# Loading and multiplying the last-but-one pair's down weights ahead of the last pair's gate-and-up weights

## Chip, cores and metric

The kernel runs on one core of one Trainium2 chip. The metric is device time in microseconds (us) of one execution. All matrix products here are in float32; TensorE is the matrix engine, VectorE and ScalarE do elementwise work, and SyncE issues nearly all loads.

## The reference

One decoder layer on 256 tokens of width 1024: a gated mixer, then a mixture of 32 experts with the best four for each token, then a final RMSNorm. The change lies in the experts:

```python
def expert_block(args):
    xb, e = args
    gu = xb @ w_gu[e] + b_gu[e]              # 1024 x 2048 weights
    gate, up = jnp.split(gu, 2, axis=-1)
    gate = jnp.minimum(gate, SWIGLU_LIMIT)
    up = jnp.clip(up, -SWIGLU_LIMIT, SWIGLU_LIMIT)
    glu = gate * jax.nn.sigmoid(SWIGLU_ALPHA * gate)
    return ((up + 1.0) * glu) @ w_down[e] + b_down[e]   # 1024 x 1024 weights
...
y_assign = ys[dest] * w_sorted[:, None]
out = jax.ops.segment_sum(y_assign, sorted_tok, num_segments=n_tok)
...
return rms_norm(x, final_g)
```

Every expert's weights are read once: 8 MB of gate-and-up and 4 MB of down weights each, 12 MB for an expert and 24 MB for a pair of them (MB here is 2^20 bytes, as in the issue sizes of the profile).

## The kernel before

The 32 experts are taken in 16 pairs, numbered 0 to 15 (`NP` is 16). The 128 rows of the matrix engine's output are four groups of 32 tokens, shared between the two experts of a pair.

For each pair the program does these steps, each a function of its own:

- `gate_up(p)` multiplies the gathered tokens with the pair's gate-and-up weights, in eight blocks k of 128 rows, into four PSUM banks, and adds the bias from two small matmuls a bank (`add_bias`).
- `swiglu(pg)` is eight VectorE operations and two ScalarE sigmoids on those banks. Its result is `act`.
- `transpose_act` turns `act` on TensorE (two groups of four transposes) and ScalarE copies each group into `actT`.
- `down(p)` multiplies `actT` with the pair's down weights; each finished bank goes through VectorE into `yv`.
- `weigh(p)` (VectorE) and `turn_weights(p)` (TensorE, ScalarE) make the matrix `owT[p]` that sends rows back to tokens, and `scatter(owT[p])` multiplies it with `yv`, piece by piece, and VectorE adds each piece to the residual stream `xt`.

All engines run their instructions in the order in which the program emits them. The order is skewed by one pair: in the loop, `weigh`, `turn_weights` and `transpose_act` of pair p-1 come first, then `gate_up(p)` (with the scatter of pair p-2 after block 0, and the gathering of the next pair's tokens between the blocks), then `swiglu` of pair p is emitted, and `down(p-1)` follows. So TensorE multiplies the down weights of pair p-1 while VectorE and ScalarE do the SwiGLU of pair p.

The weights pass through a ring of seven places of 2 MB each (`RING`, `CHUNK_ELEMS`). A chunk of two places (4 MB: two blocks k of gate-and-up weights for both experts, or half of a pair's down weights) goes into one of three double positions in turn; the seventh place is only for chunks of one place. The list of loads (`add_gu2`, `add_dn`) is issued in order by SyncE from line 177; each waits until TensorE has finished with the chunk that held its place (`passed`). Loads of pair p: four chunks of gate-and-up weights, then two chunks of the down weights of pair p-1, in whole rows: `(k, n) == (4, D)` in `dn_rows` gives four rows of 1024 floats, 16 KB in one run, to each partition.

The end differs. The down weights of pair 14 are loaded after the last gate-and-up weights, as four chunks of one place, each with half of the columns (512 floats, runs of 2 KB). `down(14, ahead)` is emitted after `swiglu` of pair 15, and `ahead` puts between its four chunks: `weigh(15)`, then the transposes of pair 15 (into a buffer `aT` of its own) and half of the scatter of pair 14, then `turn_weights(15)`. The other half of that scatter follows, then `down(15, meanwhile, aT)`, whose weights come in four chunks of one place with 512 or 256 columns in a run, and in which `meanwhile` puts the scatter of pair 15 and the sums of squares of the final norm. The rest of the final norm and the output ends the program.

The lines of the profile: 1337 is a matmul of `gate_up` or `down` (banks `abank`, `cbank`), 1354 the bias, 1304 and 1305 the transposes of `act` and their copies, 1318 and 1320 `turn_weights`, 1327 and 1270 `scatter`, 1290 to 1296 SwiGLU, 1312 `weigh`, 1393 the write of `yv`.

Of the kernel before, what the change touches and what calls it, by code (L numbers as in the profile page):

```python
# [20 lines left out]
D = 1024  # L21
KB = D // P
T = 256
TT = T // P
FF = 1024
NE = 32
TOPK = 4
NP = NE // 2
# [48 lines left out]
def trunk(ctx: ExitStack, tc: tile.TileContext, x, c, norm1_g, ada_w, ada_b, w_in, gmlp_norm_g, gmlp_ws,  # L77
# [98 lines left out]
    def load(dst, src):  # L176
        nc.sync.dma_start(dst, src)  # L177
# [101 lines left out]
    def add_dn(p, *slots):  # L279

        dn_ids[p] = []

        def fn(t, parts):
            off = 0
            for k0, k, c0, n in parts:
                for e in range(2):
                    v = t[:, off:off + k * n]
                    load(v if (k, n) == (4, D) else v.rearrange("p (k n) -> p k n", k=k), dn_rows(wdn[2 * p + e], k0, k, c0, n))
                    off += k * n
        for parts in slots:  # L290
            size = sum(2 * a[1] * a[3] for a in parts) // CHUNK_ELEMS
            i = add(lambda t, parts=parts: fn(t, parts), None, size)
            off = 0
            for a in parts:
                dn_ids[p].append((i, off, a is parts[-1]) + a)
                off += 2 * a[1] * a[3]

    for p in range(NP):
        for j in range(KB // 2):
            if (p, 2 * j) not in EXTRA:  # L300
                add_gu2(p, j)
            elif p == 0:
                for i in range(2):
                    add_gu(p, 2 * j + i)
            if (p, j) == (0, 1):
                for pk_ in EXTRA:
                    if pk_[0]:
                        add_gu(*pk_)
        if p:
            add_dn(p - 1, *([[(4 * j, 4, 0, D)] for j in range(2)] if p < NP - 1 else  # L310
                            [[(k, 4, c, 512)] for c in (0, 512) for k in (0, 4)]))
    add_dn(NP - 1, [(0, 4, 0, 512)], [(4, 2, 0, 512), (6, 2, 0, 512)], [(0, 4, 512, 256), (4, 4, 512, 256)],
           [(0, 4, 768, 256), (4, 2, 768, 256), (6, 2, 768, 256)])

# [117 lines left out]
    def half(h):  # L432
        return slice(h * 512, (h + 1) * 512)
# [601 lines left out]
    n = len(steps)  # L1035
    done = live = at = room = 0
    for i in range(n + 1):
# [5 lines left out]
        if i < n:  # L1043
# [5 lines left out]
            while spread and room >= spread[0][0]:  # L1049
                c, f = spread.pop(0)  # L1050
# [79 lines left out]
    wk = {"g2b": big.tile([P, D], F32, name="x4", bufs=2)}  # L1130
# [154 lines left out]
    def swiglu(pg, a=None):  # L1285

        a = wk["act"] if a is None else a
        gs, us_ = [wk["sg"]() for _ in range(2)], [wk["su"]() for _ in range(2)]
        for h in range(2):
            V.tensor_scalar(gs[h], pg[h], LIMIT, None, op0=OP.min)  # L1290
            S.activation(a[:, half(h)], gs[h], AF.Sigmoid, scale=ALPHA)
            V.tensor_scalar(us_[h], pg[2 + h], LIMIT, -LIMIT, op0=OP.min, op1=OP.max)
        for h in range(2):
            s, g, u = half(h), gs[h], us_[h]
            V.scalar_tensor_tensor(u, u, 1.0, g, op0=OP.add, op1=OP.mult)
            V.tensor_tensor(a[:, s], u, a[:, s], op=OP.mult)

    def transpose_act(a=None, aT=None):
        a = wk["act"] if a is None else a
        aT = wk["actT"] if aT is None else aT  # L1300
        for b in range(2):
            ps = bbank()
            for k in range(4):
                TE.transpose(ps[:, k * P:(k + 1) * P], a[:, half(b)].rearrange("p (q i) -> p i q", i=4)[:, k], ident)  # L1304
            S.activation(aT[:, 4 * b:4 * b + 4], ps.rearrange("p (k n) -> p k n", k=4), AF.Copy)

    owT = {}

    def weigh(p):

        w = ow.rearrange("p (t a g) -> p t a g", t=TT, g=GRP)
        V.tensor_tensor(w, oh[p], wg[:, :, p].unsqueeze(3).to_broadcast([P, TT, 4, GRP]), op=OP.mult)  # L1312

    def turn_weights(p):

        ps = bbank()
        for tt in range(TT):
            TE.transpose(ps[:, tt * P:(tt + 1) * P], ow[:, tt * P:(tt + 1) * P], ident)  # L1318
        owT[p] = wk["owT"]()
        S.activation(owT[p], ps[:, :T], AF.Copy)  # L1320

    def scatter(wt, c0=0, c1=D, then=None):
        for c in range(c0, c1, 512):
            n = min(512, c1 - c)
            for tt in range(TT):
                ps = bbank()[:, :n]
                TE.matmul(ps, lhsT=wt[:, tt * P:(tt + 1) * P], rhs=wk["yv"][:, c:c + n], start=True, stop=True)  # L1327
                add_rows(ps, tt, slice(c, c + n))
                if then:
                    then(tt, c, n)  # L1330
# [25 lines left out]
    def gate_up(p, during=None):  # L1356
        sel[p] = nc.values_load(isel[0:1, p:p + 1], engines=[PE], min_val=0, max_val=1,
                                skip_runtime_bounds_check_because="one minus the result of a comparison: 0 or 1")
        pg = [abank() for _ in range(4)]
        for i, k in enumerate(in_turn(p)):  # L1360
            n, row = gu_ids[p, k]
            t = chunk(n)
            ws = []
            for v in t if isinstance(t, list) else [t]:
                v = v.rearrange("p (e n) -> p e n", e=2)
                if row is not None:
                    v = v[:, :, row * 2 * FF:(row + 1) * 2 * FF]
                ws.extend(v[:, :, c:c + 512] for c in range(0, v.shape[2], 512))
            for b in range(4):
                tiles4(pg[b], xs[p % 2][:, k], lambda e: of_expert(ws[b], e, slice(0, 512)), sel[p], i == 0, False)  # L1370
            if EXTRA.get((p, k)) is None and row != 0:
                passed(n)
            if during:
                during(i)
            if i == KB - 2:
                V.tensor_copy(ex.rearrange("p (a g) -> p a g", a=4), e2g[:, p].unsqueeze(2).to_broadcast([P, 4, GRP]))
        add_bias(pg)
        return pg

    def down(p, between=None, aT=None):  # L1380
        aT = wk["actT"] if aT is None else aT
        bank = {}
        for i, (n, off, whole, k0, nk, c0, nn) in enumerate(dn_ids[p]):
            w = chunk(n)[:, off:off + 2 * nk * nn].rearrange("p (e k n) -> p e k n", e=2, k=nk)
            m = min(nn, 512)
            for kk in range(k0, k0 + nk):
                for c in range(c0, c0 + nn, m):
                    if kk == 0:
                        bank[c] = abank()[:, :m]
                    tiles4(bank[c], aT[:, kk], lambda e: of_expert(w[:, :, kk - k0], e, slice(c - c0, c - c0 + m)), sel[p],  # L1390
                           kk == 0, kk == KB - 1)
                    if kk == KB - 1:
                        V.tensor_tensor(wk["yv"][:, c:c + m], bank[c], wk["g2b"][:, c:c + m], op=OP.mult)  # L1393
            if whole:
                passed(n)
            if between:
                between(i)
# [69 lines left out]
    pg = gate_up(0, during=first)  # L1467
    work_tiles()
    swiglu(pg)
    for p in range(1, NP):  # L1470
        weigh(p - 1)
        if p > 1:
            turn_weights(p - 1)
            transpose_act()

        def during(k, p=p):
            if k == 0 and p >= 2:
                scatter(owT[p - 2])
            if k == 1 and p == 7:
                bias_down()  # L1480
            if p + 1 < NP:
                if k == 0:
                    one_hot(p + 1)
                else:
                    gather_k(p + 1, k - 1)
                if k == KB - 1:
                    gather_k(p + 1, k)
        pg = gate_up(p, during)
        if p == 1:
            more_work_tiles()  # L1490
            turn_weights(p - 1)
            transpose_act()
        swiglu(pg)
        if p == SPILL:
            tail = Carve(big.tile([P, CHUNK_ELEMS], F32, name="b2"))
            aT, scr1, scr2 = tail(FF).rearrange("p (k n) -> p k n", k=KB), tail(FF), tail(2 * FF)
            spills(scr2, scr1, xs[p % 2])
        if p < NP - 1:
            down(p - 1)


    p = NP - 1

    def ahead(i):
        if i == 0:
            weigh(p)
        if i == 1:
            transpose_act(None, aT)
            scatter(owT[p - 1], 0, 512)
        if i == 2:  # L1510
            turn_weights(p)

    def gain(tt, c, n, E):
        E.tensor_tensor(xn2[:, tt, c:c + n], xt[:, tt, c:c + n], wk["fgb"][:, c:c + n], op=OP.mult)
# [7 lines left out]
    def meanwhile(i):  # L1522
# [4 lines left out]
        if i == TB:  # L1527
            scatter(owT[p], 512, 768, finish)
            V.scalar_tensor_tensor(st[:, 48:50], st[:, 48:50], EPS, st[:, 50:52], op0=OP.add, op1=OP.add)
    down(p - 1, ahead)  # L1530
    scatter(owT[p - 1], 512)
    down(p, meanwhile, aT)
    scatter(owT[p], 768, D, finish)


# [35 lines left out]
```

## Time and profile before

| what | value |
|---|---|
| median of three runs | 1292.19 us (1291.4 to 1294.12) |
| the profiled execution | 1296.29 us, its span 1294.7 us |
| TensorE matmul busy | 1217.2 us, 94% of the span |
| DMA, mean over the span | 374 GB/s |
| granted TensorE clock, mean | 0.979 of full speed |

Busy time of a matmul row is pipelined and its ends are modelled, so 94% is not 94% of what the engine could do. A row of a timeline has the start, the time that the group took from its first start to its last end, the engine, the line, the operation and the tiles, and in brackets the idle time before it and what ended it. [...]

### The profile page before, as it was taken

How to read it: one execution, taken by the hardware profiler on the slowest of the kernel's cores; microseconds unless marked ns; L12 is line 12 of the kernel's file. 1: busy time of each engine (PE TensorE's matmuls, PEld its weight loads, DVE VectorE, ACT ScalarE, POOL GpSimd, SP SyncE). 2: the span in 40 equal slices, each digit the busy share in tenths (PEclk: the TensorE clock that was granted, in tenths of full speed). 3: DMA queues.
4: the chain of work that ended last, by engine and by line, in shares of the span. 5: the costliest groups of instructions: out<-in, count | busy, mean ns of one | idle time of the engine just before them, and what ended most of it. 6: DMA issues, size and time to landing. Idle time of an engine off the chain costs nothing. (4 is left out here: it accounts for less than half of the span.)

```text
span 1294.7 us, 22543 instructions
## 1 busy us (share of the span) xinstructions
PE 1217.2 (94%) x9653; PEld 614.1 (47%) x9654; DVE 439.9 (34%) x884; ACT 270.8 (21%) x538; POOL 11.0 (1%) x27
## 2 busy tenths in 40 slices
PE   7999999999899999898989899999989898989897
PEld 5899998999633333233333233333333333323222
DVE  3477886877431211212131223111121213121122
ACT  5564554455320000001010001000000101000011
POOL 0010000000000000000000000000000000000001
PEclk9999999999999999999999989999999999999999
DMA  9997198297798899999999989999999999999996
GB/s 342 322 386 256 49 381 296 104 390 311 258 390 360 351 427 427 427 428 428 426 426 427 427 358 429 427 426 426 427 427 427 427 427 425 420 421 427 427 389 224
DMA packets 83764, 484.72 MB, mean 374 GB/s; under 512 B 6753, under 2 KB 21161, under 8 KB 59854
## 3 DMA queue, kind: packets, MB, share of 16 engines
q1 hardware_dynamic: 82982, 481.51, 91.5%
q10 hardware_dynamic: 680, 1.71, 0.4%
q8 instruction: 80, 1.31, 0.4%
q14 instruction: 22, 0.18, 0.0%
HBM read 482.16 MB, written 1.05 MB: 373 GB/s over the span
## 5 line engine op out<-in xcount | busy, mean ns | idle before, releaser
L1337 PE MATMUL abank<-wchunk,b 128*32 (+2 forms) x4160 | 489.8, 608 | 34.9 <-DMA wchunk<-in_exp_w_down_dram 26.6
L1337 PEld LDWEIGHTS abank<-wchunk,b 128*32 128x32 f32 x4160 | 138.3, 112 | 342.4 <-issue 312.4
L1337 PE MATMUL cbank<-wchunk,b 128*32 128x512 f32 (+2 forms) x1952 | 232.5, 595 | 3.7 <-DMA wchunk<-in_exp_w_gu_dram 3.7
L1110 DVE TENSOR_SCALAR b<-bbank,a,mod 128x128 f32<-128x128 f32 x64 | 26.2, 410 | 395.9 <-PE bbank L1173 395.9
L509 DVE TENSOR_TENSOR spl<-wchunk,spl 128x512 fp32r<-128x512 f32 x196 | 132.2, 691 | 49.1 <-ACT spl L508 46.2
L1108 ACT ACTIVATE b<-bbank,mod,a 128x128 f32<-128x128 f32 x64 | 29.2, 457 | 537.9 <-PE bbank L1173 537.9
L508 ACT ACTIVATE spl<-wchunk 128x512 fp32r<-128x512 f32 x196 | 120.8, 627 | 76.3 <-PE abank L519 46.5
L516 PE MATMUL abank<-b,spl 128*128 128x256 f32 x432 | 110.3, 287 | 0.0
L1173 PEld LDWEIGHTS bbank<-spl,b 128*128 128x128 f32 x512 | 66.4, 193 | 91.4 <-issue 89.4
L517 PE MATMUL abank<-b,spl 128*128 128x256 f32 x432 | 108.3, 283 | 0.0
L1337 PEld LDWEIGHTS cbank<-wchunk,b 128*32 128x32 f32 x1952 | 55.0, 110 | 110.9 <-issue 98.1
L1173 PE MATMUL bbank<-spl,b 128*128 128x128 f32 x512 | 87.2, 300 | 1.8 <-DVE spl L1166 0.9
L516 PEld LDWEIGHTS abank<-b,spl 128*128 128x128 f32 x432 | 82.7, 191 | 3.6 <-issue 2.5
L517 PEld LDWEIGHTS abank<-b,spl 128*128 128x128 f32 x432 | 82.8, 192 | 0.2 <-issue 0.2
L1393 DVE TENSOR_TENSOR row<-abank,x 128x512 f32<-128x512 f32 (+1 forms) x32 | 21.8, 683 | 179.6 <-PE abank L1337 179.6
L1270 DVE TENSOR_TENSOR xt<-bbank,xt 128x512 f32<-128x512 f32 (+1 forms) x66 | 44.6, 675 | 107.6 <-PE bbank L1327 107.6
L519 PE MATMUL abank<-b,spl 128*128 128x256 f32 x432 | 69.7, 283 | 0.0
L1327 PE MATMUL bbank<-row,b 128*128 128x512 f32 (+1 forms) x132 | 62.7, 605 | 1.6 <-DVE row L1393 1.4
L519 PEld LDWEIGHTS abank<-b,spl 128*128 128x128 f32 x432 | 59.7, 192 | 0.0
L516 PE MATMUL cbank<-b,spl 128*128 128x256 f32 x224 | 57.2, 287 | 0.0
L517 PE MATMUL cbank<-b,spl 128*128 128x256 f32 x224 | 56.2, 283 | 0.0
L1320 ACT ACTIVATE b<-bbank 128x256 f32<-128x256 f32 x16 | 6.1, 383 | 238.5 <-PE bbank L1318 238.5
(273 smaller groups left out, 847.2 us busy)
## 6 DMA issues: line engine op xcount, KB each, us to landing
wchunk<-in_exp_w_gu_dram SPq DMA_DIRECT2D x125, 2048.0 KB, 17.3
wchunk<-in_exp_w_down_dram SPq DMA_DIRECT2D x56, 2048.0 KB, 14.6
wchunk<-in_w_in_dram SPq DMA_DIRECT2D x16, 2048.0 KB, 9.4
wchunk<-in_ada_w_dram SPq DMA_DIRECT2D x8, 2048.0 KB, 12.9
wchunk<-in_exp_w_down_dram SPq DMA_DIRECT2D x10, 1024.0 KB, 14.4
wchunk<-in_ada_w_dram SPq DMA_DIRECT2D x16, 512.0 KB, 9.5
wchunk<-in_exp_w_down_dram SPq DMA_DIRECT2D x10, 512.0 KB, 12.9
wchunk<-in_w_in_dram SPq DMA_DIRECT2D x4, 1024.0 KB, 10.5
```

What stands on the lines that cost most here:

```text
L508: S.activation(hi, w, AF.Copy)
L509: V.tensor_tensor(lo, w, hi.bitcast(F32), op=OP.subtract)
L516: TE.matmul(out_, lhsT=wh, rhs=xh, start=first and i == 0, stop=False)
L517: TE.matmul(out_, lhsT=wh, rhs=xl, start=False, stop=False)
L519: TE.matmul(out_, lhsT=wl, rhs=xh, start=False, stop=last_ and i == n - 1)
L1108: S.activation(out_, in_, AF.Identity, scale=a2[:, k:k + 1], bias=sh2[:, k:k + 1])
L1110: V.tensor_scalar(out_, in_, a2[:, k:k + 1], sh2[:, k:k + 1], op0=OP.mult, op1=OP.add)
L1173: TE.matmul(ps, lhsT=xn2[:, tt, k * P:(k + 1) * P], rhs=oh[p][:, tt].rearrange("p a g -> p (a g)"), start=tt == 0, stop=tt == TT - 1)
L1270: V.tensor_tensor(xt[:, tt, s], ps, xt[:, tt, s], op=OP.add)
L1327: TE.matmul(ps, lhsT=wt[:, tt * P:(tt + 1) * P], rhs=wk["yv"][:, c:c + n], start=True, stop=True)
L1337: TE.matmul(out_[g * GRP:(g + 1) * GRP], lhsT=xl[:, g * GRP:(g + 1) * GRP], rhs=w(e), start=start, stop=stop, skip_group_check=True)
L1393: V.tensor_tensor(wk["yv"][:, c:c + m], bank[c], wk["g2b"][:, c:c + m], op=OP.mult)
```

## The change

The list of loads for the end changes order and shape: the down weights of pair 14 come before the gate-and-up weights of pair 15, in two chunks of two places with whole rows, as for all other pairs. TensorE follows that order. After `down(13)` come `weigh(14)`, `turn_weights(14)`, `transpose_act`, the whole scatter of pair 13 and `down(14)`; then `gate_up(15)` with the scatter of pair 14 after block 0 and `weigh(15)`, `turn_weights(15)` after block 1; then `swiglu` of pair 15, `transpose_act` and `down(15, meanwhile)`. The extra buffer `aT` and the function `ahead` go; `actT` is used throughout.

```diff
     for p in range(NP):
+        if p == NP - 1:
+            add_dn(p - 1, *[[(4 * j, 4, 0, D)] for j in range(2)])
         for j in range(KB // 2):
...
-        if p:
-            add_dn(p - 1, *([[(4 * j, 4, 0, D)] for j in range(2)] if p < NP - 1 else
-                            [[(k, 4, c, 512)] for c in (0, 512) for k in (0, 4)]))
+        if 0 < p < NP - 1:
+            add_dn(p - 1, *[[(4 * j, 4, 0, D)] for j in range(2)])
...
-    def down(p, between=None, aT=None):
-        aT = wk["actT"] if aT is None else aT
+    def down(p, between=None):
+        aT = wk["actT"]
...
-    for p in range(1, NP):
+    for p in range(1, NP - 1):
...
-        if p < NP - 1:
-            down(p - 1)
+        down(p - 1)
...
     p = NP - 1
-
-    def ahead(i):
-        if i == 0:
+    weigh(p - 1)
+    turn_weights(p - 1)
+    transpose_act()
+    scatter(owT[p - 2])
+    down(p - 1)
+
+    def between(k):
+        if k == 0:
+            scatter(owT[p - 1])
+        if k == 1:
             weigh(p)
-        if i == 1:
-            transpose_act(None, aT)
-            scatter(owT[p - 1], 0, 512)
-        if i == 2:
             turn_weights(p)
+    swiglu(gate_up(p, between))
+    transpose_act()
...
-    down(p - 1, ahead)
-    scatter(owT[p - 1], 512)
-    down(p, meanwhile, aT)
+    down(p, meanwhile)
     scatter(owT[p], 768, D, finish)
```

## Rows read from the trace of the kernel before

**Rows 1.** The page: TensorE's and the DMA engines' share, and GB/s, by slice.

```profile
PE 1217.2 (94%) x9653; PEld 614.1 (47%) x9654; DVE 439.9 (34%) x884; ACT 270.8 (21%) x538; POOL 11.0 (1%) x27
...
GB/s 342 322 386 256 49 381 296 104 390 311 258 390 360 351 427 427 427 428 428 426 426 427 427 358 429 427 426 426 427 427 427 427 427 425 420 421 427 427 389 224
```

**Rows 2.** Busy time by stretch: PE, PEld, DVE, ACT, POOL, clock, DMA share, GB/s.

```profile
1139.61:1198.47 58.86, 55.18 (x439) 18.80 (x439) 11.65 (x21) 4.67 (x9) 0.00 (x0) 0.97 1.01 425
1198.47:1227.91 29.44, 26.63 (x210) 8.70 (x211) 4.62 (x8) 1.58 (x3) 0.00 (x0) 1.00 1.01 427
...
1237.66:1259.00 21.34, 21.13 (x160) 6.84 (x164) 7.48 (x12) 2.35 (x4) 0.00 (x0) 0.92 1.05 386
...
1266.00:1280.00 14.00, 14.00 (x136) 5.08 (x135) 3.45 (x5) 1.45 (x4) 1.65 (x2) 1.00 0.99 328
```

**Rows 3.** Timeline of TensorE's matmuls, from pair 13's down weights to pair 15's bias.

```profile
1198.47 7.07 PE L1337 MATMUL abank<-wchunk,b 128*32 x64 [2.53 <-DMA wchunk<-in_exp_w_down_dram]
1206.69 0.44 PE L1318 MATMUL bbank<-ident,spl 128*128 128x128 f32 x2 [1.15 <-DVE spl L1312]
...
1211.91 3.89 PE L1327 MATMUL bbank<-row,b 128*128 128x512 f32 x8
...
1227.91 1.92 PE L1337 MATMUL abank<-wchunk,b 128*32 x16 [1.67 <-DMA wchunk<-in_exp_w_gu_dram]
...
1237.66 3.20 PE L1337 MATMUL abank<-wchunk,b 128*32 x16 [2.67 <-DMA wchunk<-in_exp_w_gu_dram]
```

**Rows 4.** Timeline of TensorE's matmuls behind pair 15's bias, to its last down blocks.

```profile
1247.03 7.07 PE L1337 MATMUL abank<-wchunk,b 128*32 x64
1254.04 1.23 PE L1304 MATMUL bbank<-ident,b 128*128 128x128 f32 x8
1255.47 1.98 PE L1327 MATMUL bbank<-row,b 128*128 128x512 f32 x4 [0.21 <-ACT b L1305]
1257.38 3.64 PE L1337 MATMUL abank<-wchunk,b 128*32 x32
...
1267.69 8.80 PE L1337 MATMUL abank<-wchunk,b 128*32 x96
...
1283.03 1.93 PE L1337 MATMUL cbank<-wchunk,b 128*32 x32
```

**Rows 5.** Timeline of VectorE and ScalarE: `weigh(14)`, then the last pair's SwiGLU and transposes.

```profile
1206.22 0.42 DVE L1312 TENSOR_TENSOR spl<-spl,x 128x256 f32<-128x256 f32 x1
...
1246.89 0.69 DVE L1290 TENSOR_SCALAR b<-abank 128x512 f32<-128x512 f32 x1 [30.22 <-PE cbank L1354]
...
1250.08 0.69 DVE L1296 TENSOR_TENSOR b<-spl,b 128x512 f32<-128x512 f32 x1
...
1251.48 0.69 DVE L1296 TENSOR_TENSOR b<-spl,b 128x512 f32<-128x512 f32 x1
...
1254.82 1.08 ACT L1305 ACTIVATE b<-bbank 128x512 f32<-128x512 f32 x2 [5.37 <-PE bbank L1304]
```

**Rows 6.** Timeline of TensorE behind three idle gaps, at 541, 600 and 1073 us.

```profile
541.00 8.77 PE L1337 MATMUL abank<-wchunk,b 128*32 x64 [2.71 <-DMA wchunk<-in_exp_w_down_dram]
600.74 7.07 PE L1337 MATMUL abank<-wchunk,b 128*32 x64 [2.62 <-DMA wchunk<-in_exp_w_down_dram]
1073.25 15.64 PE L1337 MATMUL abank<-wchunk,b 128*32 x128 [3.84 <-PEq L1455]
```

**Rows 7.** Busy time by stretch behind two of those gaps, columns as in the second group.

```profile
543.00:544.00 1.00, 1.00 (x10) 0.27 (x4) 0.00 (x0) 0.00 (x0) 0.00 (x0) 0.50 1.04 442
...
1075.00:1077.00 2.00, 2.00 (x15) 0.55 (x9) 0.00 (x0) 0.00 (x0) 0.00 (x0) 0.50 0.99 418
```

**Rows 8.** Timeline of SyncE's last gate-and-up issues.

```profile
1219.44 0.80 SPq L177 DMA_DIRECT2D wchunk<-in_exp_w_gu_dram  x2
```

**Rows 9.** Weight loads of TensorE that waited in the last pair's down product.

```profile
1274.17 0.13 PEld L1337 LDWEIGHTS abank<-wchunk,b 128*32 128x32 f32 x4 [0.32 <-DMA wchunk<-in_exp_w_down_dram]
```

**Rows 10.** Busy time of the stretch in which the loads end.

```profile
1278.00:1282.00 4.00, 4.00 (x66) 2.10 (x65) 1.39 (x3) 1.45 (x4) 2.52 (x2) 1.00 0.52 170
```

More of the change, by code (lines that the diff above doesn't have):

```diff
@@ L1495, in trunk @@
             tail = Carve(big.tile([P, CHUNK_ELEMS], F32, name="b2"))
-            aT, scr1, scr2 = tail(FF).rearrange("p (k n) -> p k n", k=KB), tail(FF), tail(2 * FF)
+            scr1, scr2 = tail(FF), tail(2 * FF)
             spills(scr2, scr1, xs[p % 2])
-        if p < NP - 1:
-            down(p - 1)
+        down(p - 1)
     p = NP - 1
-    def ahead(i):
-        if i == 0:
+    weigh(p - 1)
[7 more added lines that the diff above has]
+        if k == 1:
             weigh(p)
-        if i == 1:
-            transpose_act(None, aT)
-            scatter(owT[p - 1], 0, 512)
-        if i == 2:
             turn_weights(p)
+    swiglu(gate_up(p, between))
+    transpose_act()
     def gain(tt, c, n, E):
```

## The prediction

> **What bounds the kernel now.** I read the page first. TensorE is busy for 94% of the span, but the load rate stands at 425 to 429 GB/s in nearly every slice of the second half [rows 1], so a busy TensorE alone does not say who sets the pace. The stretches settle it: from one landing of a pair's second chunk of down weights (1139.61) to the next (1198.47) pass 58.86 us at a DMA share of 1.01 and 425 GB/s [rows 2]. Those are 24 MB, or 25.17 million bytes, which take 58.9 us at 427 GB/s. So a pair costs what its loads cost, and TensorE's own work of 55.18 us in it ends in a wait for the last chunk.
>
> The timeline of the end says where this stops. TensorE starts on pair 13's second chunk the moment that it lands, at 1198.47, after 2.53 us of waiting; on the third chunk of pair 15's gate-and-up weights at 1227.91, after 1.67 us; and on the fourth and last at 1237.66, after 2.67 us [rows 3]. From 1198.47 to 1227.91 three chunks of 4 MB landed: 29.44 / 3 = 9.81 us each. After 1237.66 no matmul waits for a load again. So the time falls into two parts: up to 1237.66 the loads set it, and from there to the end, 1294.7 - 1237.66 = 57.04 us, TensorE and the final norm do, while the last 16 MB of loads run out behind them: in the stretch from 1278 to 1282 the DMA share is 0.52 [rows 10].
>
> The question for the change is therefore when the last gate-and-up chunk lands, and how much must still be done behind it.
>
> **Term 1, the landing of the last gate-and-up chunk.** Pair 14's down weights, two chunks of 4 MB, are put ahead of it. The queue is full there (DMA share 1.01 [rows 2]), so the landing moves by 2 x 9.81 = 19.62 us, to 1257.28. This needs the places in the ring to come free in time. Following the three double positions through the new list, the last chunk takes the place of the first gate-and-up chunk of pair 15, which lands where now the third does, at 1227.91. TensorE needs for its two blocks 7.1 us (from 1227.91 to the wait that begins at 1237.66 - 2.67 = 1234.99), with the scatter of pair 14 (3.89 us [rows 3]) between them: it is passed at about 1239. The chunk before the last occupies the queue until 1257.28 - 9.81 = 1247.47, so there are some 8 us to spare. Today the last chunk is issued at 1219.44 [rows 8], 18.2 us before it lands; in the new order it would be issued at the same 18 us before. SyncE's queue gets 4 issues of 2 MB instead of 8 of 1 MB, ahead of 8 gate-and-up issues; the loads of pair 15's down weights keep their shape and order. No load passes through another engine's queue here.
>
> **Term 2, what leaves the stretch behind that landing.** From 1237.66 to the start of `down(15)` at 1267.69 pass 30.03 us now [rows 3, 4]. Of these 9.37 us, to 1247.03, are the last two blocks and the bias, which stay. The remaining 20.66 us are `down(14)` (7.07 + 2 x 3.64 = 14.35 us), both halves of its scatter (2 x 1.98), eight transposes (1.23), `turn_weights(15)` (0.44) and small waits. All of these but the transposes move ahead of the new landing. They fit there. TensorE would run: `turn_weights(14)` and the transposes to 1208.3 as now, scatter of pair 13 to 1212.2, `down(14)` 2 x 7.07 to 1226.4 with its second chunk landing at 1218.1, a wait of 1.5 us, blocks 0 and 1 of pair 15 with scatter and `turn_weights` to 1239.2, blocks 2 and 3 to 1246.2, a wait to 1247.5, blocks 4 and 5 to 1254.6, a wait of 2.7 us to 1257.28. `weigh(15)` on VectorE is one short operation (0.42 us for pair 14 [rows 5], where TensorE waited 1.15 us for it [rows 3]) with a block of matmuls to hide behind, so I cost it at nothing; without that cover it is about 1 us, and it is ahead of the landing, where a wait takes it up. The removed buffer and the later `actT` cost nothing: `down(14)` read `actT` some 40 us before.
>
> **Term 3, what comes into it.** Now the SwiGLU of pair 15 runs under the 7.07 us of `down(14)`. In the new order nothing stands between: the transposes wait for `act`. VectorE starts at 1246.89 and its last product ends at 1251.48 + 0.69 = 1252.17 [rows 5], 5.14 us after the bias. The first four transposes can go at 1250.77, the last four after 1252.17 and take half of 1.23 us, so `down(15)` starts about 5.14 + 0.65 = 5.8 us after the bias, whose end I put at 1247.03, the start of what follows it now [rows 4]. If `down(15)` must also wait for the second ScalarE copy, 1.08 / 2 us come on top [rows 5]; I leave it out, because the first four blocks read only the first half, and keep it for the upper end.
>
> **Term 4, the clock.** The SwiGLU leaves TensorE idle for 1250.77 - 1247.03 = 3.7 us, and then only with transposes for 2 us. The trace has such gaps. [...] After 2.71 us, 64 took 8.77 us, 1.7 us more, at 0.50; after 2.62 us, 64 took 7.07, so the clock had stayed [rows 6, 7]. In the last pair the gap of 2.67 us before the last chunk already cost this (3.20 us for 16 matmuls that take 1.92 after the wait at 1227.91 [rows 3]), and with the new wait of 2.7 us it stays in the 9.37 us. The gap of the SwiGLU is a second one: I take 1.6 us for it. The bounds are 0 (a gap that leaves the clock alone, as the 2.62 us one) and 2.2 (the transposes, 1.23 us, slowed by half as well).
>
> [...]
>
> **The sum.** Against the profiled execution: 1257.28 (landing) + 9.37 + 5.8 + 1.6 + 27.01 (from the start of `down(15)` to the end, 1294.7 - 1267.69, unchanged) = 1301.06, which is 6.4 us more than 1294.7. In other words 19.6 us of loads come ahead of the landing, 14.9 us of work net leave the stretch behind it (20.66 less 5.8), and 1.6 us of clock are added. The profiled execution took 1296.29 us, 4.1 us above the median of the runs; the difference of 6.4 us is carried to that median: 1292.19 + 6.4 = 1298.6 us.
>
> **Rivals.**
>
> [...]
>
> The other side: the loads set the end, and the change shortens them. The end's loads in runs of 2 KB go at 386 GB/s against 427 for whole rows [rows 2]. For 8.39 million bytes that is 21.7 against 19.6 us: whole rows end all loads 2.1 us earlier. If `down(15)` waited for its loads now, by more than the SwiGLU adds, the end would follow: 1290.1 us. What decides is whether TensorE stands still for loads after 1267.69. It does not: the one such record is a weight load 0.32 us late [rows 9], its matmuls run 8.80 us for 96, which is 7.07 plus half of 3.64, and the loads cease around 1280 (half of the stretch 1278 to 1282 [rows 10]) while the last blocks start at 1283.03 [rows 4].
>
> [...]
>
> Nothing measurable. The gain and the loss of Terms 1 to 3 differ by only 4.7 us of some 20. If landings ran a little faster, the clock stayed up and both halves of the transposes went early, +2 us would remain: 1294.2.
>
> The ring runs dry. If the first gate-and-up chunk is passed later than 1247, the last one lands as much later, one for one; with 4 us beyond the spare 8, 1302.6. The timeline above speaks against it.
>
> **How the numbers follow.** A difference under 0.2% (2.6 us) can hardly be told from none here. Chances: the forecast with both clock losses 0.62; one or both of them missing 0.22; ring dry 0.05; nothing measurable 0.07; loads set the end 0.04. The first three are slower by more than 0.2%: 0.89. The range begins below the case with no clock loss by the spread of the runs (1295.4 - 0.9 = 1294.5), and ends at the forecast with the upper bounds of Terms 3 and 4 (+0.5, +0.6) and the same spread: 1300.6.
>
> **What the new profile would show.** Right: the last gate-and-up wait of TensorE ends at about 1257; behind the bias no matmul but transposes for nearly 6 us, their wait put down to VectorE's line for `act`; a stretch at 0.50 at the head of `down(15)`; no load wait after it; the loads ending near 1278 to 1281. Wrong: a last landing well before 1255 (then the queue was not full), a `down(15)` that starts less than 4 us behind the bias, or a tail from there to the end much shorter than 27 us.

## The result and the profile after

The changed kernel took 1302.5 us, the median of four runs (1297.68 to 1302.74), beside 1293.15 us for the kernel before. The ratio is 1.0058, its 95% interval 1.0034 to 1.0082: slower, as forecast, but the median lies 1.9 us above the upper end of the predicted range. The profiled execution took 1297.68 us, with a span of 1296.0 us.

So the two profiled spans differ by 1.3 us and the medians by 9.4. Neither is the price of the change. To see the price, I measure the end from a moment that both kernels share: the start of TensorE on pair 13's second down chunk, up to which the work is the same. It is 1198.47 us in the profile before [rows 3] and 1193.19 us in this one. From there to the end of the span: 1294.7 - 1198.47 = 96.2 us before, 1296.0 - 1193.19 = 102.8 us after.

The stretches between landings, after (columns as in [rows 2]; the clock there is the granted one, as a share of full speed):

```profile
1193.19:1222.88 29.69, 26.50 (x211) 8.59 (x212) 5.86 (x9) 1.58 (x3) 0.00 (x0) 1.00 1.01 427
1222.88:1252.28 29.40, 25.48 (x202) 7.89 (x203) 3.23 (x6) 0.38 (x1) 0.00 (x0) 1.00 1.00 419
1252.28:1270.00 17.72, 13.34 (x88) 4.99 (x92) 5.07 (x8) 3.76 (x6) 0.00 (x0) 0.81 1.01 348
1270.00:1280.00 10.00, 10.00 (x104) 3.46 (x100) 1.83 (x3) 0.70 (x2) 0.54 (x1) 1.00 0.28 93
```

The queue stays full to 1252.28 (DMA shares of 1.01 and 1.00), where the last gate-and-up chunk lands. TensorE's timeline, after, answers to [rows 3, 4]:

```profile
1193.19 7.07 PE L1338 MATMUL abank<-wchunk,b 128*32 x64 [2.63 <-DMA wchunk<-in_exp_w_down_dram]
...
1206.90 13.94 PE L1338 MATMUL abank<-wchunk,b 128*32 x128
1222.88 1.92 PE L1338 MATMUL cbank<-wchunk,b 128*32 x16 [2.04 <-DMA wchunk<-in_exp_w_gu_dram]
...
1252.28 3.28 PE L1338 MATMUL cbank<-wchunk,b 128*32 x16 [2.74 <-DMA wchunk<-in_exp_w_gu_dram]
...
1265.45 0.75 PE L1305 MATMUL bbank<-ident,b 128*128 128x128 f32 x4 [3.73 <-DVE b L1297]
1266.85 1.13 PE L1305 MATMUL bbank<-ident,b 128*128 128x128 f32 x4 [0.65 <-DVE b L1297]
1267.90 9.70 PE L1338 MATMUL abank<-wchunk,b 128*32 x96
```

Here is what is new: idle times of 3.73 and 0.65 us whose releaser is line 1297, the last product of SwiGLU on VectorE, and a head of `down(15)` whose 96 matmuls take 9.70 us where they took 8.80 [rows 4]. The same stretch by slices of the clock, after:

```profile
1262.00:1264.00 2.00, 0.00 (x0) 0.00 (x0) 2.00 (x5) 1.19 (x2) 0.00 (x0) 1.00 1.01 338
...
1266.00:1268.00 2.00, 1.35 (x10) 0.83 (x13) 0.69 (x1) 0.60 (x1) 0.00 (x0) 0.59 1.06 357
1268.00:1270.00 2.00, 2.00 (x12) 0.50 (x16) 0.00 (x0) 1.90 (x3) 0.00 (x0) 0.56 1.10 344
1270.00:1272.00 2.00, 2.00 (x24) 0.60 (x20) 0.00 (x0) 0.18 (x1) 0.00 (x0) 1.00 0.93 306
```

VectorE is busy for the whole first slice and TensorE for none of it; in the next two rows shown TensorE works at a granted clock of 0.59 and 0.56.

### The profile page after: what moved, and what is told of

Same layout as the page of the kernel before. It is cut to its first block, busy times and chain, and to the rows that moved or that the text cites. A ratio compares the mean times of both kernels' runs of the same rounds, so it can differ in the third digit from the quotient of the medians.

```text
span 1296.0 us, 22538 instructions
## 1 busy us (share of the span) xinstructions
PE 1206.8 (93%) x9653; PEld 613.6 (47%) x9654; DVE 439.9 (34%) x884; ACT 271.0 (21%) x538; POOL 11.0 (1%) x27
## 3 DMA queue, kind: packets, MB, share of 16 engines
q10 hardware_dynamic: 680, 1.71, 0.4%
## 5 line engine op out<-in xcount | busy, mean ns | idle before, releaser
L1338 PE MATMUL abank<-wchunk,b 128*32 (+2 forms) x4160 | 480.5, 598 | 32.1 <-DMA wchunk<-in_exp_w_down_dram 27.3
L1174 PEld LDWEIGHTS bbank<-spl,b 128*128 128x128 f32 x512 | 65.3, 190 | 91.2 <-issue 89.3
L1174 PE MATMUL bbank<-spl,b 128*128 128x128 f32 x512 | 86.0, 297 | 2.0 <-DVE spl L1167 0.9
```

The lines of the kernel that those rows point to most:

```text
L1174: TE.matmul(ps, lhsT=xn2[:, tt, k * P:(k + 1) * P], rhs=oh[p][:, tt].rearrange("p a g -> p (a g)"), start=tt == 0, stop=tt == TT - 1)
L1338: TE.matmul(out_[g * GRP:(g + 1) * GRP], lhsT=xl[:, g * GRP:(g + 1) * GRP], rhs=w(e), start=start, stop=stop, skip_group_check=True)
```

## The experiments

Every run below gives a profile, so two readings stand side by side: the ratio to the kernel before on the same chip, and the end's stretch. Times in the table are in us from the start on pair 13's second down chunk; the landing is that of the last gate-and-up chunk. Each row is one profiled execution; only the changed kernel (seven in all, with the four further down) and the kernel before (two) have more than one. Where no granted clock is shown, I read a fall of the clock from the matmuls. In the profile before, with a clock of 1.00 beside them, 64 take 7.07 us (from 1198.47 [rows 2, 3]), 96 take 8.80 (from 1267.69 [rows 2, 4]) and 16 take 1.92 (from 1227.91 [rows 3]); behind the wait of 2.67 us, with 0.50 from 1238.66 to 1240.66, 16 take 3.20.

| kernel | landing | `down(15)` starts | end | ratio (95% interval) |
|---|---|---|---|---|
| before, the profile shown | 39.2 | 69.2 | 96.2 | |
| before again | 39.2 | 69.0 | 96.2 | 1.0002 (0.9991 to 1.0012) |
| changed, the profile shown | 59.1 | 74.7 | 102.8 | 1.0058 (1.0034 to 1.0082) |
| changed, second set | 58.8 | 74.4 | 102.6 | 1.0061 (1.0045 to 1.0076) |
| changed, third set | 58.9 | 74.4 | 102.3 | 1.0064 (1.0047 to 1.0081) |
| changed, no SwiGLU of pair 15 | 59.0 | 69.9 | 97.1 | 1.0006 (0.9995 to 1.0018) |
| changed, idle gap filled | 58.8 | 74.1 | 101.3 | 1.0062 (1.0046 to 1.0078) |
| changed, half rows ahead | 60.8 | 74.7 | 102.7 | 1.0058 (1.0044 to 1.0072) |
| half of the move | 49.0 | 69.0 | 96.1 | 0.9997 (0.9984 to 1.0009) |
| before, whole rows, two chunks | 39.1 | 73.3 | 100.5 | 1.0047 (1.0033 to 1.0061) |
| before, wait filled | 39.3 | 67.6 | 96.1 | 0.9990 (0.9979 to 1.0002) |
| before, runs of 8 KB | 39.2 | 66.6 | 94.5 | 0.9982 (0.9970 to 0.9994) |
| before, runs of 8 KB, wait filled | 39.2 | 66.6 | 94.3 | 0.9986 (0.9975 to 0.9998) |

**The changed kernel again, twice, and the kernel before against itself.** No edit.

> The changed kernel once more. Theory (the end alone): from the start of TensorE on pair 13's second down chunk to the end of the span, 102.8 us as in its first profile (96.2 us in the profile of before), whatever the whole span is; time about 6.5 us over before, 1.0050. Rival (something ahead of the end also became slower by the change): the stretch up to that start is longer than before's 1198 us in the profile, and the time is 9 to 10 us over before, 1.0072.

> The changed kernel a third time. Theory (the change costs 6.5 us in the end's stretch, and what a run's time shows besides is scatter ahead of it that the change does not touch): 102.6 to 102.8 us from pair 13's second down chunk to the end if the clock falls twice there, ratio 1.005 to 1.006. Rival (the change also slows the kernel ahead of the end): ratio 1.007 or more.

> The kernel before against itself. Theory: ratio 1.000 within its interval; 96.2 us from pair 13's second down chunk to the end, or 94.6 plus waits for loads where the clock does not fall; the start of that stretch anywhere from 1193 to 1201 us, as in the profiles of all kernels so far. Rival (the start of that stretch belongs to the kernel): 1198 us again.

The end's stretch came as expected, but for the third set's 102.3, which is 0.3 us below its range. The ratios, 1.0061 and 1.0064, lie between my figures and the rival's (1.0050 and 1.0072 in the second set, at most 1.006 and at least 1.007 in the third), and their intervals hold both: they do not decide. The rival's cause did not show: the changed kernel's stretch begins at 1194.20 and 1194.44 us, earlier than the 1195.54 of the kernel before, whose own two profiles differ by 3 us here (1198.47 the first time). What makes that start vary is read further down, and it is the same in both kernels.

**SwiGLU left out.**

```diff
-    swiglu(gate_up(p, between))
+    gate_up(p, between)
     transpose_act()
```

> The changed kernel with pair 15's SwiGLU left out: its transposes take pair 14's act, so the output is another one. Theory (the exposed SwiGLU and the clock fall behind it are the price): both go, 102.8 - 4.4 (idle 3.73 and 0.65) - 1 to 1.6 (clock) = 97 us from pair 13's second down chunk to the end, and the time comes to within 1 us of before, ratio 0.999 to 1.001. Rival (the later landing is paid for by itself, since too little work moved ahead of it): it stays 3 us or more over before.

The output is another one, so this kernel serves only to price the SwiGLU. The end is 97.1 us, and the ratio is 1.0006. The timeline shows the transposes directly behind the bias, and a head of 8.80 us, as at a clock of 1.00:

```profile
1262.93 1.23 PE L1305 MATMUL bbank<-ident,b 128*128 128x128 f32 x8
1264.43 8.80 PE L1338 MATMUL abank<-wchunk,b 128*32 x96 [0.27 <-ACT b L1306]
```

So the bare SwiGLU with its clock fall is 102.8 - 97.1 = 5.7 us of the price, and the later landing, less the work moved ahead of it, about 1 us. The rival falls. The ratios give the SwiGLU somewhat more, 0.0055 of 1293 us or 7.1 us against the changed kernel's second set.

**The idle gap filled.**

```diff
     swiglu(gate_up(p, between))
+    keep_clock(12, bbank)
     transpose_act()
```

> The changed kernel with 12 matmuls of 128 x 128 of no use between the last bias and the transposes, some 3.4 us in the idle 3.73 us. Theory (the gap costs a second clock fall): the head of the last down product runs at 1.00, its 96 matmuls in 8.8 us for 9.7, and 1 us is won against the changed kernel, 1.0042 to before. Rival (the clock falls anyway, from the wait before the last chunk, or the fall is cheap): no change against the changed kernel, within 0.3 us in the end's stretch.

The 12 matmuls stand as 24 in the profile, two for each.

```profile
1262.15 2.94 PE L103 MATMUL bbank<-ones,ident 128*128 128x128 f32 x24
1265.96 0.75 PE L1305 MATMUL bbank<-ident,b 128*128 128x128 f32 x4 [0.86 <-DVE b L1297]
1267.45 0.72 PE L1305 MATMUL bbank<-ident,b 128*128 128x128 f32 x4 [0.74 <-DVE b L1297]
1268.10 8.80 PE L1338 MATMUL abank<-wchunk,b 128*32 x96
```

The second transposes take 0.72 us for 1.13 and the head 8.80 for 9.70, so the clock stays up, and the end is 101.3 us, 1.0 to 1.5 us less than in the three changed profiles of the table. The ratio, 1.0062 where 1.0042 was expected, cannot tell this from nothing. A part of the reason is on record: in the six runs of this kernel the time is 2.2 to 2.7 us longer than the span of the core's instructions, in the changed kernel's six of the same set 1.5 to 1.6. By the medians of the spans (1297.1 against 1298.25 us) 1.1 us are won, and some 0.9 us of that are lost outside the span, where no profile looks.

**Half of the move.** The first 4 MB of pair 14's down weights ahead, the rest behind, so that half of `down(14)` again lies under the SwiGLU.

```diff
-            add_dn(p - 1, *[[(4 * j, 4, 0, D)] for j in range(2)])
+            add_dn(p - 1, [(0, 4, 0, D)])
...
+            add_dn(p - 1, [(4, 2, 0, D)], [(6, 2, 0, D)])
...
-    down(p - 1)
+    down(p - 1, None, slice(0, 1), banks14)
...
     swiglu(gate_up(p, between))
-    transpose_act()
+    down(p - 1, None, slice(1, 3), banks14)
+    transpose_act(None, aT)
+    scatter(owT[p - 1])
```

> Half of the move: the first 4 MB of pair 14's down weights in whole rows ahead of pair 15's gate-and-up weights and multiplied there, the other 4 MB behind them in two chunks of one place (runs of 8 KB), multiplied while SwiGLU of pair 15 runs; then its transposes (into a buffer of their own) and the scatter of pair 14. Theory (each 4 MB ahead costs 9.81 us of landing and takes only its matmuls away; the rest of the loss is the bare SwiGLU, here covered again): last landing 49.0 us behind the start on pair 13's second down chunk, and from that start to the end 49.0 + 9.4 + 7.1 + 1.4 + 3.8 + 27.0 = 97.8 us, 1.5 us over before's 96.2, ratio 1.001. Rival (the loss grows with the bytes moved, SwiGLU or not): half of the changed kernel's 6.5, so 99.5 us, ratio 1.0025.

The landing is at 49.0 us as worked out. The end is 96.1 us and the ratio 0.9997: no loss at all. It is 1.7 us under my sum because the clock did not fall at the last chunk (16 matmuls in 1.92 us): the timeline has the fall one chunk earlier (16 in 3.27), where there was a wait behind it to take it up (1.11 us are left of that wait).

```profile
1237.18 3.27 PE L1342 MATMUL cbank<-wchunk,b 128*32 x16 [2.63 <-DMA wchunk<-in_exp_w_gu_dram]
...
1247.07 1.92 PE L1342 MATMUL cbank<-wchunk,b 128*32 x16 [1.11 <-DMA wchunk<-in_exp_w_gu_dram]
...
1254.74 7.07 PE L1342 MATMUL abank<-wchunk,b 128*32 x64
1261.74 1.23 PE L1309 MATMUL bbank<-ident,b 128*128 128x128 f32 x8
```

The rival, a loss in proportion to the bytes moved, falls: its ratio of 1.0025 lies outside the interval, and half the bytes cost nothing that 12 runs could show once the SwiGLU is covered.

**Half rows ahead.**

```diff
-            add_dn(p - 1, *[[(4 * j, 4, 0, D)] for j in range(2)])
+            add_dn(p - 1, *[[(k, 4, c, 512)] for c in (0, 512) for k in (0, 4)])
```

> The changed kernel with pair 14's down weights in four chunks of half rows (runs of 2 KB) as in the kernel before, but still ahead of pair 15's gate-and-up weights. Theory (the landing of the last gate-and-up chunk sets the end): 8.39 million bytes at 386 for 427 GB/s land 2.1 us later, 104.7 us from pair 13's second down chunk to the end, ratio 1.007. Rival (TensorE's work sets it): as the changed kernel, 102.6 us.

The last landing moved as forecast, from 58.8 to 59.1 us in the changed kernel to 60.8. The end did not: 102.7 us. Behind the longer wait for the first gate-and-up chunk (3.84 us, 2.04 in the profile after) the clock fell, with 16 matmuls in 2.88 us; the last chunk's blocks ran at 1.92 us for 16, so 1.7 us came back (from its landing to the bias 7.0 us for 8.7):

```profile
1227.33 2.88 PE L1338 MATMUL cbank<-wchunk,b 128*32 x16 [3.84 <-DMA wchunk<-in_exp_w_gu_dram]
...
1256.64 1.92 PE L1338 MATMUL cbank<-wchunk,b 128*32 x16 [2.34 <-DMA wchunk<-in_exp_w_gu_dram]
```

By its total this run does not decide between the theories; by its landing it bears out the slower rate of the 2 KB runs: 1.7 to 2.0 us more for the 8.39 million bytes, where 386 for 427 GB/s [rows 2] make 2.1.

**Whole rows at the old place.** The shape alone, in the kernel before.

```diff
-            add_dn(p - 1, *([[(4 * j, 4, 0, D)] for j in range(2)] if p < NP - 1 else
-                            [[(k, 4, c, 512)] for c in (0, 512) for k in (0, 4)]))
+            add_dn(p - 1, *[[(4 * j, 4, 0, D)] for j in range(2)])
...
         if i == 1:
             transpose_act(None, aT)
+            turn_weights(p)
             scatter(owT[p - 1], 0, 512)
-        if i == 2:
-            turn_weights(p)
```

> The kernel before with only the shape changed: pair 14's down weights stay behind the last gate-and-up weights, but in two chunks of whole rows; the transposes of pair 15 and the first half of the scatter stand behind the second chunk. Theory (TensorE sets the end, not the loads): the loads end 2 us earlier, about 1278 in a span like before's, and the time stays within 1 us of before, ratio 0.9995 to 1.0008. Rival (the loads set the end): 2 us faster, 0.9984.

Both theories missed: it is slower, 1.0047, and the end is 100.5 us. The timeline says why:

```profile
1247.85 7.07 PE L1336 MATMUL abank<-wchunk,b 128*32 x64 [0.44 <-DMA wchunk<-in_exp_w_down_dram]
1257.65 8.77 PE L1336 MATMUL abank<-wchunk,b 128*32 x64 [2.73 <-DMA wchunk<-in_exp_w_down_dram]
```

The loads do end earlier (DMA share 0.51 already in the stretch from 1276 to 1280), but a chunk of 4 MB must land whole before its first matmul. TensorE now waits for both, and behind the second wait the clock falls (8.77 us for 64 matmuls that take 7.07 behind the first): 0.44 + 2.73 + 1.70 us, of which 4.2 us reach the end. The ratio gives 6.1 us, with 4.3 at the lower end of its interval. The four chunks of 2 MB of the kernel before let it start on a quarter of the weights. My statement that no load matters after the last gate-and-up chunk was true of that kernel only by a small margin, and the next run measures it.

**The wait ahead of the last chunk filled, in the kernel before.**

```diff
+            if k == KB - 3 and p == NP - 1:
+                keep_clock(8, bbank)
```

> The kernel before with 8 matmuls of no use behind block 5 of pair 15's gate-and-up weights, some 2.3 us in the wait of 2.67 us ahead of the last chunk. Theory A (TensorE alone sets the end): the clock stays at 1.00, 1.6 us are won, 94.6 us from pair 13's second down chunk to the end, ratio 0.9988. Theory B, the one that the run with whole rows of pair 14 points to (the loads of the end come just in time): most of the 1.6 us come back as waits for the down weights of pair 15, and the end stays at 95.8 to 96.2, ratio 0.9995 to 1.0000.

```profile
1233.84 1.92 PE L1337 MATMUL abank<-wchunk,b 128*32 x16 [0.76 <-DMA wchunk<-in_exp_w_gu_dram]
...
1262.17 7.20 PE L1337 MATMUL abank<-wchunk,b 128*32 x64
1270.15 1.93 PE L1337 MATMUL abank<-wchunk,b 128*32 x32 [0.78 <-DMA wchunk<-in_exp_w_down_dram]
...
1276.07 1.93 PE L1337 MATMUL cbank<-wchunk,b 128*32 x32 [0.21 <-DMA wchunk<-in_exp_w_down_dram]
```

The clock held (16 matmuls in 1.92 us), `down(15)` began 1.6 us earlier, and waits for its own weights took nearly all of it back: 96.1 us. By the profile theory B holds. The ratio, 0.9990, lies nearer theory A's 0.9988, and its interval (0.9979 to 1.0002) holds both.

**Runs of 8 KB in chunks of one place, without and with that filling.**

```diff
-                            [[(k, 4, c, 512)] for c in (0, 512) for k in (0, 4)]))
+                            [[(k, 2, 0, D)] for k in (0, 2, 4, 6)]))
...
         if i == 1:
             transpose_act(None, aT)
-            scatter(owT[p - 1], 0, 512)
-        if i == 2:
+        if i == 3:
             turn_weights(p)
...
-    scatter(owT[p - 1], 512)
+    scatter(owT[p - 1])
```

> The kernel before with pair 14's down weights in four chunks of one place as before, but of two whole rows for each partition (runs of 8 KB) instead of half rows; transposes of pair 15 behind the second chunk, the whole scatter of pair 14 behind the fourth. Theory (whole rows in two places lost 4.2 us because 4 MB must land at once, not because of their shape): no wait for pair 14's weights, 96.0 to 96.9 us from pair 13's second down chunk to the end, ratio 1.000. Rival (the order of the work behind is what cost): 99 to 100 us again, ratio 1.003.

> Both: runs of 8 KB in chunks of one place and the 8 matmuls ahead of the last gate-and-up chunk. Theory (the faster loads of 8 KB runs let TensorE keep what the clock gives): 94.6 to 95.2 us from pair 13's second down chunk to the end, ratio 0.9990. Rival (no gain from the loads): as with the 8 matmuls alone.

The ends are 94.5 and 94.3 us, the ratios 0.9982 and 0.9986; the first is 1.5 us under its forecast. The first kernel's timeline:

```profile
1234.08 1.92 PE L1337 MATMUL abank<-wchunk,b 128*32 x16 [2.62 <-DMA wchunk<-in_exp_w_gu_dram]
...
1274.77 1.93 PE L1337 MATMUL cbank<-wchunk,b 128*32 x32 [0.24 <-DMA wchunk<-in_exp_w_down_dram]
```

Small chunks with longer runs remove the loss of the 4 MB chunks and let the end keep what the clock gives. The last wait for pair 15's down weights ends 79.9 us after the shared start here (1274.77 - 1194.92) and 79.7 in the second kernel. In the run above, with the wait filled and runs of 2 KB, it ended at 81.5 (1276.07 - 1194.59). So the loads land 1.6 to 1.8 us earlier, and the end gains as much on that run. The order of the scatter of pair 14, which this edit moves as well, lets `down(15)` begin 1.0 us earlier (66.6 for 67.6); what that is worth by itself was not run. In the first of the two the clock happened to stay up by itself in the profiled execution (16 matmuls in 1.92 us after a wait of 2.62, at 1.00 from 1234 to 1256), so the two profiles say nothing about the filling; nor do the ratios. Both beat the kernel before, by 0.14 to 0.18%, and the changed kernel by more.

**Four more executions of the changed kernel.** No edit. Half of its 16 runs in the three sets lay at 1302 to 1305 us, and all three profiles near 1298.

> The changed kernel, one profiled look, to catch an execution of 1302 us or more. Theory (scatter ahead of the end): TensorE starts on pair 13's second down chunk about 4 us later than in the executions of 1298 us (1194), and the end from there is 102.3 to 102.8 us again. Rival (the end itself has a slower form): the start is at 1194 and the end takes 106 us or more.

> The changed kernel, a second look. Theory and rival with their numbers as for the first look: a start 4 us later and an end of 102.3 to 102.8 us, or a start at 1194 us and an end of 106.

> The changed kernel, a third look. Theory and rival with their numbers as for the first look: a start 4 us later and an end of 102.3 to 102.8 us, or a start at 1194 us and an end of 106.

> The changed kernel, a fourth look. Theory and rival with their numbers as for the first look: a start 4 us later and an end of 102.3 to 102.8 us, or a start at 1194 us and an end of 106.

| execution | time | stretch begins | `down(15)`'s first 96 matmuls | end |
|---|---|---|---|---|
| first | 1299.55 | 1193.86 | 11.14 | 104.1 |
| second | 1301.47 | 1197.49 | 11.15 | 102.3 |
| third | 1297.93 | 1193.59 | 9.77 | 102.7 |
| fourth | 1301.69 | 1195.97 | 11.26 | 104.1 |

Neither theory holds alone. The two executions above 1301 us begin the end 2 to 4 us later, as the theory says, and in three of the four the head of `down(15)` loses 2.3 to 2.5 us to the clock (11.14 to 11.26 us for 8.80) where the profiled one lost 0.9. The slices at the head in the second execution:

```profile
1268.00:1270.00 2.00, 1.54 (x8) 1.07 (x7) 1.03 (x2) 0.60 (x1) 0.00 (x0) 0.55 0.93 302
1270.00:1272.00 2.00, 2.00 (x14) 0.44 (x16) 0.00 (x0) 1.57 (x2) 0.00 (x0) 0.50 1.03 344
1272.00:1274.00 2.00, 2.00 (x16) 0.55 (x12) 0.00 (x0) 0.51 (x2) 0.00 (x0) 0.50 1.09 355
1274.00:1276.00 2.00, 2.00 (x16) 0.44 (x12) 0.00 (x0) 0.00 (x0) 0.00 (x0) 0.74 1.05 332
```

Here the gap of 3.72 us was no longer than in the profile above, and the clock stayed at 0.50 for the whole of two slices and parts of the next ones on either side. Where the earlier loss lies, one stretch near the start of the experts shows, in the second execution and then in the third:

```profile
340.00:360.00 20.00, 16.87 (x133) 7.75 (x133) 6.83 (x20) 3.78 (x7) 0.00 (x0) 0.91 0.53 152
```

```profile
340.00:360.00 20.00, 17.43 (x149) 8.13 (x153) 7.38 (x26) 3.16 (x6) 0.00 (x0) 1.00 0.60 192
```

The same text of the same kernel: once the clock falls there, with 133 matmuls and 152 GB/s in these 20 us, once it does not, with 149 and 192. The second execution reaches the stretch 0.6 us behind the third and is 1.6 us behind at 540 us. Another such place lies near 750 us, again in the second execution and then in the third:

```profile
750.00:760.00 10.00, 10.00 (x76) 3.11 (x72) 0.41 (x1) 0.46 (x1) 0.00 (x0) 0.86 0.60 229
```

```profile
750.00:760.00 10.00, 10.00 (x88) 3.67 (x91) 0.41 (x1) 0.92 (x2) 0.00 (x0) 1.00 0.77 292
```

There the lag grows from 2.8 us, at 719 us, to the 3.9 us that it has from 840 us on and at the start of the end's stretch (1197.49 - 1193.59); the 1.2 us that it gains between 540 and 719 us stay unplaced. In both places the load rate is lower too (152 for 192 and 229 for 292 GB/s), and the lost time is not made good afterwards. Neither place belongs to the change. In the profile of the kernel before:

```profile
340.00:360.00 20.00, 16.71 (x130) 7.76 (x133) 6.62 (x23) 4.17 (x8) 0.00 (x0) 0.91 0.54 147
...
750.00:760.00 10.00, 10.00 (x75) 3.07 (x71) 0.36 (x1) 0.46 (x1) 0.00 (x0) 0.83 0.58 242
```

The profiles with a timeline of both places, 15 of the 17, sort by them. In the first, a fall shows in eight matmuls near 343 us (L1173 before, L1174 in the changed kernel): 1.71 to 2.05 us for 1.13. In the second, it shows in the first 16 matmuls on `abank` from 747 us on: 2.34 to 2.67 us for 1.89 to 2.02. Without a fall in either (seven profiles), the end's stretch begins between 1193.2 and 1194.9 us; with a fall in the first alone (three) between 1195.5 and 1196.0; with a fall in both (five) between 1197.5 and 1200.7. Kernels with the old and with the new order of the end stand in each of the three groups. The profile shown of the kernel before had both falls and that of the changed kernel none. With that goes a start 5.3 us later, which hides all but 1.3 us of the 6.6 between their ends when whole spans are compared.

## Why the prediction was right in kind and off in size

**Term 1** held. The landing was forecast 58.8 us after the shared start (1257.28 - 1198.47) and measured at 58.8 to 59.1 in seven profiles, with half the bytes ahead at 49.0. The ring had room.

**Term 2** held. In the profile after, the moved work is done when the last chunk lands, and TensorE waits 2.74 us for it (2.7 forecast).

**Term 3** held. From the landing to `down(15)`: 9.37 + 5.8 = 15.2 us forecast, 15.6 measured (1267.90 - 1252.28), of which the waits of 3.73 and 0.65 us are the SwiGLU; the 0.4 us over are transposes at the lower clock (0.59 from 1266 to 1268; Term 4). `down(15)` did not wait for the second copy. With the SwiGLU left out, the end returned to within 1 us of before; this is the one part of the price that the experiments pin most firmly.

**Term 4** was mis-sized. I took 1.6 us for the second clock fall, an estimate between the 1.5 us that I read behind the gap of 3.84 us (15.64 less 2 x 7.07 [rows 6]) and the 1.7 behind that of 2.71, with 2.2 as the upper bound. No run shows 1.6 us as a fixed price. At the head of `down(15)`, where 96 matmuls take 8.80 us at a granted clock of 1.00 [rows 2, 4], the seven profiles lost 0.6 to 2.5 us behind the same gap of 3.7 us, and the second transposes another 0.4 (1.13 us for four, where the run with the gap filled has 0.72). That is 1.0 to 2.9 us, 1.9 on average, so the term was 0.3 us short on average and its upper bound too low in three executions of seven. I had treated one gap's price in one profile as a constant, and under-read it: behind the gap of 3.84 us, 128 matmuls took 15.64 us, and at a granted clock of 1.00 128 take 13.94 (`down(14)` in the profile after), not 2 x 7.07, so that gap cost 1.7 us.

**The sum** for the end's stretch was 102.6 us (96.2 + 6.4). The seven profiles give 102.3 to 104.1, 103.0 on average, against 96.2 in both profiles of before: 6.8 us.

**The step that failed is the one that carried the 6.4 us to a median and put a spread of 0.9 us around it.** The median of 1292.19 us stood on three runs; 86 runs of the kernel before give 1290.9 to 1297.4 with a median of 1293.8. The sign was in hand: the prediction's own profiled execution lay 4.1 us above that median, and I took 0.9 us for the spread all the same. The first four runs of the changed kernel fell on its high side: all 20 spread from 1297.7 to 1304.8 with a median of 1300.9. Those two displacements are 1.6 us each, and make 10.3 us (1302.5 - 1292.19) of what is 7.1 us between the medians of all runs. So of the 3.9 us between forecast and result, 3.2 are the choice of runs on the two sides, which is chance as far as the record shows, and 0.7 are the sum. A range with a spread of 3 us on either side would just have held the result.

Between 6.8 us in the profiles and 7.1 us (or 0.0061 and 0.0064 of 1293 us in the two larger sets, 7.9 and 8.3 us) some 0.3 to 1.5 us stay without a place. No profile shows an execution of the changed kernel above 1302 us, so it remains open whether those lose the rest ahead of the end and at the clock, as the two near 1301.5 us did, or elsewhere. Nothing new is needed for them: a start of 1193.2 to 1198.8 us (all profiles but one at 1200.7), an end of 102.3 to 104.1 and 1.6 us outside the span add up to 1297.1 to 1304.5, beside runs of 1297.7 to 1304.8. The granted clock on record points the same way without proving it: 0.980 on average in the eight runs above 1302 us, 0.984 in the other twelve.

**The rivals.** The case with no clock loss, from which my range begins (1295.4 us, the forecast less 1.6 us for each of two falls), did not occur in a whole execution, though in the second of the four later ones the fall at the last chunk was missing (16 matmuls in 1.92 us). That the ring runs dry did not occur. The rival on the other side, loads that set the end, was rightly rejected for this change, but closer than I wrote: I read one weight load 0.32 us late [rows 9] as no wait. As a delay it is next to nothing, since the weight loads around it start after 0.30 us of idle time without waiting for a load. It was the sign that the down weights of pair 15 arrived just in time, and 1.6 us won ahead of them came to nothing until the loads were made faster too.

## What to carry to other kernels

At the end of a pipeline, ask what each piece of work covers, not only what it costs: the down product that was moved ahead was the cover of a chain on two other engines, and half of it was cover enough. Where weights arrive just in time, the size of a chunk decided more here than the length of its runs, since a chunk must land whole: an end of 100.5 us with 4 MB chunks against 94.5 with 2 MB ones, of which the clock fall at the last gate-and-up chunk, absent in the second, is 1.7 us (from its landing to the bias 8.7 us against 7.0). The DMA engines were full with either size (a share of 1.04 from 1270 to 1276 us with the 4 MB chunks, of 1.01 and 1.02 from 1234 to 1266 with the 2 MB ones), and it was the matmuls that started sooner. And price a change from a moment that both profiles share to the end: the spans of the two profiles of the kernel before differ by 3.0 us, their ends by 0.1.

## What was not expected of the hardware

The same idle gap of TensorE, 3.7 us, cost the matmuls behind it between 0.6 and 2.5 us in seven executions of one program, and gaps of 2.0 to 3.1 us ahead of 64 matmuls cost 1.4 to 1.7 us (8.43 to 8.77 us for 7.07) or nothing. The shortest that cost it, in the changed kernel's third set, stands beside the gap of 2.04 us at 1222.88 in the profile after, which cost nothing:

```profile
1194.44 8.77 PE L1338 MATMUL abank<-wchunk,b 128*32 x64 [2.04 <-DMA wchunk<-in_exp_w_down_dram]
```

A fall ahead of a wait for loads was free: in four of the seven executions this chunk took 8.77 us instead of 7.07, and the last landing still came 58.8 to 59.1 us after its start, as in the other three. And in one run a wait of 3.84 us early in the end went with a fall there and none at the last chunk, where it would have counted: where the clock falls can matter more than how often.
